# Running the first feed-forward block of the first tile on x·g, with the norm factor applied after the sums, and x and the first weights loaded first

## The chip, the cores and the metric

The kernel runs on all 8 cores of one Trainium2 chip. Each core computes one batch element with its own copy of the program. The time is device time in microseconds of the slowest core. Most executions of one kernel agree closely (the kernel before, seven in one batch: 2812.6 to 2815.0 us), but some fall into a slower state in which the cores of one die (0 to 3, or 4 to 7), sometimes of both, show a lower granted TensorE clock. In one of 3333.07 us, for example, cores 4 to 7 had a mean clock of 0.819 to 0.826, and cores 0 to 3 of 0.992 to 0.994. This text compares undisturbed executions only. Where a trace contains both kinds of core, it uses the undisturbed ones.

## The reference, cut to what matters

```python
D_MODEL, BATCH, SEQ, D_FF = 1024, 8, 4096, 2816

def rmsnorm(x, g):
    y = x * lax.rsqrt(jnp.mean(x * x, axis=-1, keepdims=True) + EPS)
    return y * g

def swiglu(h, w_gate, w_up, w_down):
    return (jax.nn.silu(h @ w_gate) * (h @ w_up)) @ w_down

# x: (8, 4096, 1024) float32
x = x + 0.5 * swiglu(rmsnorm(x, norm_ffn1), ffn1_w_gate, ffn1_w_up, ffn1_w_down)
h = rmsnorm(x, norm_mix)
... # attention branch and spatial-gating ("sgu") branch from h @ w_in, merged by gates
x = x + merged @ w_out
x = x + 0.5 * swiglu(rmsnorm(x, norm_ffn2), ffn2_w_gate, ffn2_w_up, ffn2_w_down)
return rmsnorm(x, norm_final)
```

The norm factor is one number per row of x, so `(x*r*g) @ w` equals `r * ((x*g) @ w)`. That identity is what the change uses.

## The kernel before: the parts that matter

Each core walks over 8 tiles of 512 rows. The weights are float32 in HBM. They arrive through a ring in SBUF, in chunks of up to 1 MB of bf16. A chunk is first loaded with a DMA that casts float32 to bf16, issued by GpSimd. In some tile it is written back to HBM as bf16, and later loads are plain copies issued by SyncE:

```python
def pump():                                     # fills the ring, in the order of use
    ...
    if chunk not in converted:
        u = uses.get(chunk, 0); uses[chunk] = u + 1
        ...
        p.dma("pool", lambda e, ...: e.dma_start(out=dst, in_=src), writes=res, ...)   # casts
        if u >= (first_seen[chunk] * 2) % NREP:                                        # NREP = 3
            converted.add(chunk)
            pending_wb[k] = (chunk, scr, dst, i)     # written back when it is first used
    else:
        p.dma("sp", lambda e, ...: e.dma_start(out=dst, in_=scr), ...)                  # plain
```

For the 19 chunks of the first FFN (11 of gate and up weights, 8 of down weights), this rule writes back 7 chunks in tile 0, 6 in tile 1 and 6 in tile 2.

The norm adds up eight squares and turns the sum into a factor RSTD with one matmul and two ScalarE operations.

```python
def nsq(t, d, eng="pool"):     # square on ScalarE; the running sum ACC on `eng`, GpSimd by default
    ...
    p.add("act", ... AF.Square ...)
    if d < 7:
        p.add(eng, lambda e: e.tensor_tensor(out=ACC[:], in0=ACC[:], in1=buf[:], op=ALU.add), ...)
    else:
        p.add("dve", ... out=ACCR[:] ...)
```

The FFN takes its PSUM banks in pairs, and the pieces of other work ("hooks") run between the groups of matmuls. Four of the eight banks serve all dense products in turn:

```python
def dense_bank():
    b = dn[0] % 4; dn[0] += 1; return b

for f2 in (3, 8, 9, 10, 2, 0, 1, 4, 5, 6, 7):        # 11 weight chunks
    Wc, wres, k = get_slot(("ffs", i, f2))
    for a in range(2):                               # two pairs per chunk
        bg, bu = dense_bank(), dense_bank()
        ...                                          # 8 gate matmuls into bg
        ...                                          # silu: ScalarE (tanh form in the second FFN)
        hook()
        ...                                          # 8 up matmuls into bu
        ...                                          # VectorE: HT = silu(gate) * up
        hook()
...                                                  # then 8 chunks of the down projection

def sgu_mix(t, s):                                   # one of the hooks
    b = dense_bank()                                 # takes the next bank for 8 small matmuls
```

The start of the program, and the hooks of the first FFN of tile 0:

```python
for d in range(8): nsq(0, d, "dve")
nstat()
for d in range(8): napply(0, 0, d)                   # XT = x * g * RSTD
run_all(ffn(0, 0, False, ffn1_hooks(0)))

add_hook(hk, 4, const_loads); add_hook(hk, 8, P(load_x, 1))      # constants, x of tile 1
for i in range(4): add_hook(hk, 20 + 2 * i, P(bias_exp, i))
add_hook(hk, 30, const_ops)                          # 9 us of set-up on VectorE
```

Of the kernel before, what the change touches and what calls it, by code (L numbers as in the profile page):

```python
# [181 lines left out]
def build_nc(n_tiles=NT):  # L182
# [28 lines left out]
    with ExitStack() as st:  # L211
# [5 lines left out]
        def bank(i):  # L217
            return PS[i // 2][:, (i % 2) * 512:(i % 2 + 1) * 512]
# [54 lines left out]
        def run(p, dry):  # L273
# [29 lines left out]
            def pump():  # L303
                while nxt[0] < len(chunk_order) and (general[0] or nxt[0] < fast_len[0]):
                    k = nxt[0]
                    chunk = chunk_order[k]
                    scr, src, ncols = chunk_aps(chunk)
                    ng = -(-ncols // 512)
                    o = cursor[0]
                    if o + ng > NGR:  # L310
                        o = 0
                    if any(a < o + ng and o < b for a, b in live.values()):
                        return
                    nxt[0] += 1
                    cursor[0] = o + ng
                    live[k] = (o, o + ng)
                    res = [("rg", g) for g in range(o, o + ng)]
                    dst = RING[:, o * 512:o * 512 + ncols]
                    W = dst
                    place[k] = (W, res)  # L320
                    if len(scr.shape) == 3:
                        dst = dst.rearrange("p (f c) -> p f c", f=scr.shape[1])
                    i = k % NSEM
                    if chunk not in converted:
                        u = uses.get(chunk, 0)
                        uses[chunk] = u + 1
                        if chunk not in first_seen:
                            first_seen[chunk] = len(first_seen)
                        p.dma("pool", lambda e, dst=dst, src=src: e.dma_start(out=dst, in_=src),
                              writes=res, sem=f"slotq{i}")  # L330
                        if u >= (first_seen[chunk] * 2) % NREP:
                            converted.add(chunk)
                            pending_wb[k] = (chunk, scr, dst, i)
                    else:
                        p.dma("sp", lambda e, dst=dst, scr=scr: e.dma_start(out=dst, in_=scr),
                              reads=[("SCR", chunk)], writes=res, sem=f"slot{i}")
# [28 lines left out]

            dn = [0]

            def dense_bank():
                b = dn[0] % 4
                dn[0] += 1  # L370
                return b

# [89 lines left out]
            def napply(t, which, d):  # L462
# [4 lines left out]
                    out=dst, in0=src, scalar=G4[:, which * 8 + d:which * 8 + d + 1], in1=RSTD[:], op0=ALU.mult, op1=ALU.mult),  # L467
                    reads=[xres, "RSTD", "G4"], writes=[dres])

            def store(t, d):  # L470
                b = t % 3
                p.dma("sp", lambda e: e.dma_start(out=out_d[:, d:d + 2, t * T:(t + 1) * T], in_=X[b][:, d:d + 2, :]),
                      reads=[("X", b, d), ("X", b, d + 1)], writes=[("outd", d)], sem=f"o{d}")

            N_FFN = 2 * NFC + 16

            def ffn(t, i, use_tanh, hooks=None):
                hooks = hooks or {}
                xt, xp, b3 = XT[t % 2], t % 2, t % 3
                piece = 0  # L480

                def hook():
                    nonlocal piece
                    if piece in hooks:
                        hooks[piece]()
                    piece += 1

                for f2 in (3, 8, 9, 10, 2, 0, 1, 4, 5, 6, 7):
                    Wc, wres, k = get_slot(("ffs", i, f2))
                    for a in range(2):  # L490
                        fc = 2 * f2 + a
                        W = Wc[:, a * 2048:(a + 1) * 2048]
                        bg, bu = dense_bank(), dense_bank()
                        for kc in range(8):
                            p.add("pe", lambda e, kc=kc, W=W, bg=bg: e.matmul(  # L495
                                bank(bg), lhsT=W[:, kc * 128:(kc + 1) * 128], rhs=xt[:, kc, :], start=(kc == 0), stop=(kc == 7)),
                                reads=wres + [("XT", xp, kc)], writes=[rb(bg)])
                        buf, bres = tg_buf()
                        if use_tanh:
                            p.add("act", lambda e, buf=buf, bg=bg: e.activation(out=buf[:], in_=bank(bg), func=AF.Tanh, scale=0.5),  # L500
                                  reads=[rb(bg)], writes=[bres])
                            p.add("dve", lambda e, buf=buf, bg=bg: e.scalar_tensor_tensor(  # L502
                                out=buf[:], in0=buf[:], scalar=1.0, in1=bank(bg), op0=ALU.add, op1=ALU.mult),
                                reads=[bres, rb(bg)], writes=[bres])
                        else:
                            p.add("act", lambda e, buf=buf, bg=bg: e.activation(out=buf[:], in_=bank(bg), func=AF.Silu),  # L506
                                  reads=[rb(bg)], writes=[bres])
                        hook()
                        yield
                        for kc in range(8):  # L510
                            p.add("pe", lambda e, kc=kc, W=W, bu=bu: e.matmul(  # L511
                                bank(bu), lhsT=W[:, 1024 + kc * 128:1024 + (kc + 1) * 128], rhs=xt[:, kc, :],
                                start=(kc == 0), stop=(kc == 7)),
                                reads=wres + [("XT", xp, kc)], writes=[rb(bu)])
                        p.add("dve", lambda e, buf=buf, bu=bu, fc=fc: e.tensor_tensor(  # L515
                            out=HT[:, fc, :], in0=bank(bu), in1=buf[:], op=ALU.mult),
                            reads=[rb(bu), bres], writes=[("HT", fc)])
                        if a == 1:
                            free_slot(k)
                        hook()  # L520
                        yield
                fac = 0.25 if use_tanh else 0.5
                for d in range(8):
                    W, wres, k = get_slot(("wds", i, d))
                    by = dense_bank()
                    for part in range(2):
                        for fc in range(part * 11, part * 11 + 11):
                            p.add("pe", lambda e, fc=fc, W=W, by=by: e.matmul(  # L528
                                bank(by), lhsT=W[:, fc * 128:(fc + 1) * 128], rhs=HT[:, fc, :],
                                start=(fc == 0), stop=(fc == NFC - 1)),  # L530
                                reads=wres + [("HT", fc)], writes=[rb(by)])
                        if part == 1:
                            xs = X[b3][:, d, :]
                            p.add("dve", lambda e, by=by, xs=xs: e.scalar_tensor_tensor(  # L534
                                out=xs, in0=bank(by), scalar=fac, in1=xs, op0=ALU.mult, op1=ALU.add),
                                reads=[rb(by), ("X", b3, d)], writes=[("X", b3, d)])
                            free_slot(k)
                        hook()
                        yield
# [347 lines left out]
            def ffn1_hooks(t):  # L887
                hk = {}
                if t == 0:
                    add_hook(hk, 4, const_loads)  # L890
                    add_hook(hk, 30, const_ops)
                    for i in range(4):
                        add_hook(hk, 20 + 2 * i, P(bias_exp, i))
                    add_hook(hk, 8, P(load_x, 1))
                    for d in range(8):
                        add_hook(hk, 16 + 3 * d, P(nsq, 1, d))
                    add_hook(hk, 52, bias_sums)
                    add_hook(hk, 41, nstat)
                    for d in range(8):
                        add_hook(hk, 43 + d, P(napply, 1, 0, d))  # L900
                if t == 1:
                    add_hook(hk, 0, nstat)
                    for d in range(8):
# [32 lines left out]
            def run_all(g):  # L936
                for _ in g:
                    pass

            load_x(0)  # L940
            p.dma("act", lambda e: e.dma_start(out=G4[:], in_=g4_d), writes=["G4"], sem="c0")
            if not dry:
                pump()
            p.add("dve", lambda e: e.memset(ONESR[:].bitcast(F32), 1.0), writes=["ONESR"])
            p.add("dve", lambda e: e.memset(EPSB[:], EPS), writes=["EPSB"])
            p.add("dve", lambda e: e.memset(NHALF[:], -0.5), writes=["NHALF"])
            for d in range(8):
                nsq(0, d, "dve")
            nstat()
            for d in range(8):  # L950
                napply(0, 0, d)
            run_all(ffn(0, 0, False, ffn1_hooks(0)))

            nxt_ffn = ffn(1, 0, True, ffn1_hooks(1))
            for _ in range(4):
# [154 lines left out]
```

## Time and profile before

| | before |
|---|---|
| time, median of the 3 fast runs beside the changed kernel | 2814.84 us |
| TensorE share of the chain that ended last (core 0; 91% on core 5) | 92% |
| first matmul of the first FFN | 24.4 us |
| first FFN of tile 0 done | 163.2 us |
| steady tile (a later tile, measured from a fixed point in it to the same point in the next) | 342.2 us |

The profiled execution of this kernel: cores 0 to 3 had a mean granted clock of 0.93, cores 4 to 7 of 0.994 to 0.995. Cores 4 to 7 took 2802.6 to 2810.0 us here; in seven fast executions of this kernel the same cores took 2800.8 to 2813.5, so they stand for an undisturbed run. All readings below are of core 5. The page (of the slow core 0) says in its part on the chain that ended last (work followed back from the last instruction, so a share of the span and not of busy time):

```profile
PE 92%; DMA 3%; DVE 2%; ACT 1%; issue 1%; POOL 0%; DVEq 0%; ACTq 0%; SPq 0%; POOLq 0%
```

On core 5 the same part gives 91% to TensorE and 4% to DMA. So the program is bound by TensorE. What can be won lies in its gaps. The waits view of TensorE, core 5, names what matmuls waited for (line, releaser: us in total, times, longest):

```profile
PE ps L455 <- DVE ACCR L447: 31.7, 11, 21.1
...
PE ps L495 <- DMA RING<-fsrc: 6.2, 3, 3.8
...
PE ps L511 <- DVE HT L515: 4.7, 2, 2.6
PE ps L495 <- ACT TG L506: 4.3, 2, 3.3
```

The 21.1 us is the start: TensorE has nothing to do until the squares of x are summed. The timeline of TensorE, core 5, shows it (start, duration, line, operation, count; in brackets the idle time before it and what ended that):

```profile
21.14 0.77 PE L455 MATMUL ps<-ACCR,ONESR 128*128 128x512 f32 x1 [21.14 <-DVE ACCR L447]
24.42 5.22 PE L495 MATMUL ps<-XT,RING 128*128 128x512 bf16 x8 [2.52 <-DVE XT L466]
...
35.93 1.89 PE L495 MATMUL ps<-XT,RING 128*128 128x512 bf16 x8
...
107.41 3.45 PE L511 MATMUL ps<-XT,RING 128*128 128x512 bf16 x8 [2.65 <-DVE HT L515]
...
124.75 21.53 PE L528 MATMUL ps<-HT,RING 128*128 128x512 bf16 x99
...
163.19 1.89 PE L495 MATMUL ps<-XT,RING 128*128 128x512 bf16 x8
```

The first chunk runs from 24.4 to 35.9 us, partly at a slow pace. The down projection starts at 124.75 us and the first FFN is done at 163.19 us. A group of eight matmuls takes 1.89 us in most of the trace, but the one at 107.41, after a wait of 2.65 us, takes 3.45: its matmuls start 0.43 us apart instead of 0.216. At the start the spacing of 0.43 us holds from 29.4 to 32.0 us; there the granted clock reads 1.00, so the trace shows the pace but not what sets it. The eight matmuls before that start 0.66 us apart, which is the pace at which VectorE writes XT (eight tiles in 5.39 us), so their spacing is VectorE's and not TensorE's own.

One write-back looks expensive. The chain that ended last, core 5, has this piece (start, duration, what):

```profile
46.21 40.46 DMA ffs<-RING
```

A write-back of 1 MB took 40 us from issue to landing (the median of the 22 such write-backs on this core is 12.5 us), and its ring slot was held for that time.

### The profile page before, as it was taken

To read this page: it belongs to the slowest core of one execution; us is meant where nothing else is said; L and a number is where in the kernel's file an instruction comes from. 1 tells how busy PE (TensorE), PEld (TensorE's weight loads), DVE (VectorE), ACT (ScalarE), POOL (GpSimd) and SP (SyncE) were. 2 spreads that over 40 slices of the span, in tenths; PEclk is the share of its full clock that TensorE was granted. 3 is DMA by queue.
4 is the path that set the end of the run, shared out by engine and by line. 5 is a ranking of instruction groups with operands and counts; after the bars stand their busy time and mean duration, and the time that the engine had idled before them with its cause. 6 is when DMAs were issued, how large, how long until landed. Compare 5 with 4: busy or idle time off the path is not lost.

```text
span 2974.2 us, 38345 instructions; the slowest of 8 cores (2802.6 to 2974.2 us)
## 1 busy us (share of the span) xinstructions
PE 2891.8 (97%) x13034; PEld 1288.2 (43%) x13034; DVE 1248.1 (42%) x1929; ACT 893.9 (30%) x1347; POOL 503.3 (17%) x490
## 2 busy tenths in 40 slices
PE   6899999999999999999999999999999999999997
PEld 2344444444444444444444444444444444444443
DVE  2326343263432644336433464324544255455432
ACT  2323232232322323224232232323323233343221
POOL 0212312112111121111211121111211112102111
PEclk9899889998999999999999999999999999999998
DMA  9988999877777554664344443444334443433352
GB/s 194 189 166 209 176 182 176 176 208 175 176 185 184 169 144 154 176 202 170 133 142 144 161 149 135 149 144 164 139 137 140 144 148 133 141 128 123 128 182 78
DMA packets 112517, 472.41 MB, mean 159 GB/s; under 512 B 9144, under 2 KB 9144, under 8 KB 104128
## 3 DMA queue, kind: packets, MB, share of 16 engines
q1 hardware_dynamic: 90288, 371.71, 36.4%
q0 software_dynamic: 21312, 97.10, 20.6%
q8 instruction: 112, 1.84, 0.2%
q10 hardware_dynamic: 720, 1.07, 0.2%
q14 instruction: 85, 0.70, 0.1%
HBM read 501.92 MB, written 65.01 MB: 191 GB/s over the span
## 4 chain that ended last, share of the span: by engine, by line
PE 92%; DMA 3%; DVE 2%; ACT 1%; issue 1%; POOL 0%; DVEq 0%; ACTq 0%; SPq 0%; POOLq 0%
PE ps L528 22%; PE ps L511 20%; PE ps L495 20%; PE ps L810 8%; PE ps L557 6%; PE ps L820 4%; PE ps L570 3%; PE ps L839 3%; PE ps L701 2%; PE ps L687 2%; DMA ffs<-RING 1%; DMA RING<-fsrc 1%; DMA wos<-RING 0%; PE ps L644 0%; PE ps L455 0%
## 5 line engine op out<-in xcount | busy, mean ns | idle before, releaser
L495 PE MATMUL ps<-XT,RING 128*128 128x512 bf16 x2816 | 706.7, 396 | 6.8 <-DVE XT L466 2.5
L511 PE MATMUL ps<-XT,RING 128*128 128x512 bf16 x2816 | 706.8, 397 | 6.3 <-DVE HT L515 6.3
L528 PE MATMUL ps<-HT,RING 128*128 128x512 bf16 x2816 | 660.7, 399 | 0.0
L528 PEld LDWEIGHTS ps<-HT,RING 128*128 128x128 bf16 x2816 | 285.2, 102 | 362.7 <-issue 145.2
L515 DVE TENSOR_TENSOR HT<-ps,TG 128x512 bf16<-128x512 f32 x352 | 241.1, 685 | 466.8 <-PE ps L511 419.0
L511 PEld LDWEIGHTS ps<-XT,RING 128*128 128x128 bf16 x2816 | 281.4, 101 | 351.3 <-issue 121.2
L495 PEld LDWEIGHTS ps<-XT,RING 128*128 128x128 bf16 x2816 | 281.8, 101 | 350.5 <-issue 119.6
L444 POOL TENSOR_TENSOR ACC<-ACC,TG 128x512 f32<-128x512 f32 x186 | 239.8, 1289 | 1075.4 <-ACT TG L441 1074.3
L441 ACT ACTIVATE TG<-X 128x512 f32<-128x512 f32 x224 | 140.2, 627 | 547.5 <-DVE X L534 453.4
L534 DVE SCALAR_TENSOR_TENSOR X<-ps,X 128x512 f32<-128x512 f32 x128 | 88.4, 692 | 424.7 <-PE ps L528 420.8
L810 PE MATMUL ps<-XT,RING 128*128 128x512 bf16 x1024 | 261.1, 401 | 0.0
L506 ACT ACTIVATE TG<-ps 128x512 f32<-128x512 f32 x176 | 105.0, 597 | 449.0 <-PE ps L495 435.4
L691 ACT ACTIVATE E<-ps 128x1024 bf16<-128x1024 f32 (+1 forms) x240 | 168.4, 702 | 197.3 <-PE ps L687 174.3
L732 POOL TENSOR_SCALAR TG<-TG 128x512 bf16<-128x512 f32 x64 | 98.8, 1543 | 587.3 <-DVE TG L721 577.6
L502 DVE SCALAR_TENSOR_TENSOR TG<-TG,ps 128x512 f32<-128x512 f32 x176 | 119.7, 680 | 168.5 <-ACT TG L500 145.3
L500 ACT ACTIVATE TG<-ps 128x512 f32<-128x512 f32 x176 | 105.1, 597 | 266.6 <-PE ps L495 236.1
L557 PE MATMUL ps<-XT,RING 128*128 128x512 bf16 x768 | 178.2, 395 | 0.0
L694 DVE TENSOR_TENSOR E<-E,EB 128x1024 bf16<-128x1024 bf16 (+1 forms) x240 | 127.5, 531 | 94.9 <-ACT E L691 93.9
L824 DVE SCALAR_TENSOR_TENSOR TG<-TG,ps 128x512 f32<-128x512 f32 x128 | 87.8, 687 | 182.1 <-PE ps L820 155.3
L810 PEld LDWEIGHTS ps<-XT,RING 128*128 128x128 bf16 x1024 | 103.8, 102 | 135.1 <-issue 60.2
L815 ACT ACTIVATE TG<-ps,BG 128x512 f32<-128x512 f32 x128 | 87.5, 687 | 241.1 <-PE ps L810 241.0
L466 DVE SCALAR_TENSOR_TENSOR XT<-X,G,RSTD 128x512 bf16<-128x512 f32 x192 | 135.6, 746 | 30.9 <-ACT RSTD L459 30.9
(91 smaller groups left out, 1937.5 us busy)
## 6 DMA issues: line engine op xcount, KB each, us to landing
RING<-ffs SPq DMA_DIRECT2D x131, 1024.0 KB, 5.0
RING<-wds SPq DMA_DIRECT2D x97, 704.0 KB, 4.4
RING<-fsrc POOLq DMA_DIRECT2D x45, 1024.0 KB, 13.4
RING<-mgs SPq DMA_DIRECT2D x48, 768.0 KB, 4.3
RING<-wis SPq DMA_DIRECT2D x29, 1024.0 KB, 4.8
ffs<-RING SPq DMA_DIRECT2D x22, 1024.0 KB, 12.2
RING<-wd POOLq DMA_DIRECT2D x31, 704.0 KB, 11.2
out<-X SPq DMA_DIRECT2D x32, 512.0 KB, 4.1
```

Of the source, the lines that this page charges most:

```text
L441: p.add("act", lambda e: e.activation(out=buf[:], in_=src, func=AF.Square, scale=1.0 / 32.0), reads=[xres], writes=[bres])
L444: p.add(eng, lambda e: e.tensor_tensor(out=ACC[:], in0=ACC[:], in1=buf[:], op=ALU.add), reads=["ACC", bres], writes=["ACC"])
L466: p.add("dve", lambda e: e.scalar_tensor_tensor(out=dst, in0=src, scalar=G4[:, which * 8 + d:which * 8 + d + 1], in1=RSTD[:], op0=ALU.mult ...
L495: p.add("pe", lambda e, kc=kc, W=W, bg=bg: e.matmul(bank(bg), lhsT=W[:, kc * 128:(kc + 1) * 128], rhs=xt[:, kc, :], start=(kc == 0), stop= ...
L502: p.add("dve", lambda e, buf=buf, bg=bg: e.scalar_tensor_tensor(out=buf[:], in0=buf[:], scalar=1.0, in1=bank(bg), op0=ALU.add, op1=ALU.mul ...
L511: p.add("pe", lambda e, kc=kc, W=W, bu=bu: e.matmul(bank(bu), lhsT=W[:, 1024 + kc * 128:1024 + (kc + 1) * 128], rhs=xt[:, kc, :], start=(k ...
L515: p.add("dve", lambda e, buf=buf, bu=bu, fc=fc: e.tensor_tensor(out=HT[:, fc, :], in0=bank(bu), in1=buf[:], op=ALU.mult), reads=[rb(bu), b ...
L528: p.add("pe", lambda e, fc=fc, W=W, by=by: e.matmul(bank(by), lhsT=W[:, fc * 128:(fc + 1) * 128], rhs=HT[:, fc, :], start=(fc == 0), stop= ...
L557: p.add("pe", lambda e, kc=kc, W=W, b=b, cc=cc: e.matmul(bank(b), lhsT=W[:, kc * 512 + cc * 128:kc * 512 + (cc + 1) * 128], rhs=XT[t % 2][ ...
L691: p.add("act", lambda e: e.activation(out=ee, in_=PS[2][:].rearrange("p (h c) -> p h c", h=2)[:, :, 0:n], func=AF.Exp), reads=[rb(4), rb(5 ...
L694: p.add("dve", lambda e: e.tensor_tensor(out=ee, in0=ee, in1=EB[:, 2 * hp:2 * hp + 2, u0:u0 + n], op=ALU.mult), reads=[("E", i % 2), ("EB" ...
L810: p.add("pe", lambda e, kc=kc, W=W, bgt=bgt, j=j: e.matmul(bank(bgt), lhsT=W[:, j * 1024 + kc * 128:j * 1024 + (kc + 1) * 128], rhs=XT[t % ...
```

## The change

Intent: chunk 0 of tile 0's first FFN runs k by k on x·g as x lands, with no norm before it. The norm factor scales the sums as they leave PSUM: VectorE multiplies the gate sums by RSTD, ScalarE applies silu, VectorE multiplies by RSTD again, and the product with the up sums follows. x and the first weight chunk are loaded first, the latter in four quarters. No chunk is written back in tile 0. Set-up work moves later, and so do the squares, the norm factor and x·g of tile 1 (not shown below). The raw FFN turns over six PSUM banks instead of four.

```diff
+                        if k == 0:                       # first chunk in four quarters
+                            for j in range(4): ...
+                        else:
+                            p.dma("pool", ...,
+                                  reads=[("X", 0, 7)] if k == 1 else (), writes=res, ...)   # waits for x
-                        if u >= (first_seen[chunk] * 2) % NREP:
+                        if u >= (first_seen[chunk] % 2 + 1 if first_seen[chunk] < 19 else (first_seen[chunk] * 2) % NREP):
...
+            def nraw(t, which, d): ...                   # XT = x * g
...
+                    elif raw:
+                        p.add("dve", ... out=buf[:], in0=bank(bg), in1=RSTD[:], op=ALU.mult ...)
+                        p.add("act", ... out=buf[:], in_=buf[:], func=AF.Silu ...)
+                        p.add("dve", ... out=buf[:], in0=buf[:], in1=RSTD[:], op=ALU.mult ...)
...
+                n_dense[0] = 6 if raw else 4
                 for f2 in (3, 8, 9, 10, 2, 0, 1, 4, 5, 6, 7):
+                    by_k = raw and f2 == 3
+                    banks = [dense_bank() for _ in range(4)]
+                    if by_k:
+                        for kc in range(8):
+                            nraw(t, 0, kc)
+                            for j in range(4): mm(banks[j], Wc, wres, j, kc)
+                            ...
                     for a in range(2):
-                        bg, bu = dense_bank(), dense_bank()
+                        bg, bu = banks[2 * a], banks[2 * a + 1]
...
-                    add_hook(hk, 4, const_loads)
+                    add_hook(hk, 20, const_loads)
-                        add_hook(hk, 20 + 2 * i, P(bias_exp, i))
+                        add_hook(hk, 36 + 2 * i, P(bias_exp, i))
-                    add_hook(hk, 8, P(load_x, 1))
+                    add_hook(hk, 14, P(load_x, 1))
...
-            for d in range(8):
-                nsq(0, d, "dve")
-            nstat()
-            for d in range(8):
-                napply(0, 0, d)
-            run_all(ffn(0, 0, False, ffn1_hooks(0)))
+            run_all(ffn(0, 0, False, ffn1_hooks(0), raw=True))
```

Note the line `banks = [...]`: it is needed for the k-by-k chunk, but it stands in the code of every FFN of every tile.

## The prediction

> All readings are of core 5 (clock 0.995; die 0 was slow in the profiled run).
>
> **What bounds the kernel.** TensorE. In the waits view its matmuls wait about 39 us in the first tile's first FFN (0 to 163 us) and almost nothing from 180 to 530 us. Those 39 us: 21.1 us before the first matmul (the norm's sums; x lands over 18.7 us because five weight casts share the DMA), 2.5 us for the norm factor, 6.2 us for weights, 4.3 and 4.7 us for evictions held up by setup work. The first matmuls go at 0.66, then 0.43 us each instead of 0.216 us[...]. DMA share is mostly 0.9 to 1.04 over the first 200 us. From queue bytes over queue share, a casting weight chunk (1 MB) costs about 6.5 us, a plain megabyte 2.7 us; TensorE uses a chunk in 6.9 us.
>
> **What the change does.**
> 1. No norm wait: chunk 0 runs by k as x lands. I expect the first matmul at 11-15 us, chunk 0 done at 20-23 us (before: 36). Gain there about 15 us.
> 2. No write-backs in tile 0. Before, one took 40 us (46 to 86 us, chain of waits) and held a ring slot. This goes.
> 3. Against it: later chunks start only when x has landed, and the second x tile and bias table (3.9 MB with the constants), no longer behind a write-back, compete with chunks 1 to 3. I expect waits there, chunk 3 at about 46 us.
> 4. Every gate costs VectorE three 0.69 us operations around one 0.60 us ScalarE one, in order: about 3.2 us per pair, against 3.46 us of matmuls. No slack remains for setup. The constant setup (9.6 us of VectorE, 97 to 106.6 us before) waits for the small spatial-gating weights, now queued behind chunk 9 (estimate: landing at 84-90 us). After it four bias exponentials, each with two 1.28 us table loads, stretch four pairs to about 5.3 us. From the setup's end the chain needs 0.7 + 6.4 + 21.2 us, then 35 us of down projection: first FFN done at 157-165 us, against 163-166 before. Most of the early gain is given back.
> 5. Tile 1: seven chunks that came back as bf16 are casts again, with four more write-backs: about 31 us more DMA work. Before, I count 141 us of DMA work from 163 to 330 us; after, about 172. The ring's five chunks should hide this; up to 5 us of weight waits possible. Tile 2 gets about 16 us more, into idle DMA.
>
> **On the critical path:** the first 163 us; nothing later unless the DMA falls behind.
>
> **Prediction:** 2809 us, range 2796 to 2819 (before: 2814.84). Faster by over 2% 0.01, within 2% 0.97, slower by over 2% 0.02. Even removing all 39 us would be 1.4%.
>
> **What would show each step.** Timeline: first matmul near 11-15 us; chunk 0's end. Waits: matmuls on weights for chunks 1 to 3. Groups: two new norm-factor multiplications, 22 each, near 0.69 us. Timeline: constant setup starting at 80-90 us, TensorE then waiting on VectorE; the down projection's first bank waiting for the last hidden rows. Windows: DMA share near 1 from 165 to 330 us.
>
> **What would make it wrong.** If the small weights land early, or table loads overlap better, the first FFN ends near 150 us and the gain is 10 to 18 us. If the extra casts in tile 1 make TensorE wait, the result is 10 us or more slower; write-backs could also hold ring slots there as in tile 0.

## More of the kernel before

A ruler for the rest: the first matmul of the gates' merge (line 810) occurs once per tile. Its start on core 5 in tiles 0 and 2:

```profile
330.97 1.89 PE L810 MATMUL ps<-XT,RING 128*128 128x512 bf16 x8
...
1015.42 1.89 PE L810 MATMUL ps<-XT,RING 128*128 128x512 bf16 x8
```

Below, **T0** is the start of the first merge, **D1** and **D2** the next two distances from merge to merge (here 342.3 and 342.2), and a **steady tile** one of the later ones (342.2). Tile 0's first FFN lies in T0, and most of the repeated weight casts in T0, D1 and D2.

## The result, and the profile after

The changed kernel took 2842.66 us (median of 4 runs, 2841.12 to 2845.6, all undisturbed) against 2814.84 us (median of the 3 fast runs of before). The ratio is 1.0099, with a 95% interval of 1.0079 to 1.0119: some 28 us slower, outside the predicted range and with the wrong sign. The result was correct. All ratios here are the mean time of one kernel's fast runs over that of the other's of the same rounds, so not quite the ratio of the medians quoted.

The same view of the chain that ended last, on the slowest core (2):

```profile
PE 84%; DMA 9%; DVE 2%; ACT 2%; issue 2%; POOL 0%; SPq 0%; ACTq 0%; DVEq 0%; POOLq 0%
```

DMA rose from 3% (4% on core 5) to 9% of the chain. The waits view of TensorE, core 2:

```profile
PE ps L504 <- DMA RING<-fsrc: 29.3, 6, 13.9
PE ps L464 <- DVE ACCR L456: 21.6, 10, 9.8
PE ps L571 <- DVE TG L517: 11.3, 1, 11.3
...
PE ps L504 <- DVE HT L527: 6.0, 1, 6.0
PE ps L687 <- ACT TG L523: 5.7, 6, 0.9
...
PE ps L687 <- DVE TG L513: 3.6, 2, 1.8
```

The wait for the sum of squares at the start is gone. In its place are 29.3 us of waits for weights, 13.86 of them before the first matmul, and two waits of 6 and 11 us behind VectorE. A norm wait of 9.8 us belongs to a later tile. The two L687 rows (the small matmuls of sgu_mix) are new: their 9.3 us have no counterpart in before. (Line numbers differ between the two kernels.) The timeline of TensorE, core 2:

```profile
13.86 0.59 PE L504 MATMUL ps<-XT,RING 128*128 128x512 bf16 x1 [13.86 <-DMA RING<-fsrc]
...
23.25 8.64 PE L504 MATMUL ps<-XT,RING 128*128 128x512 bf16 x29 [3.71 <-DMA RING<-fsrc]
...
37.17 22.97 PE L504 MATMUL ps<-XT,RING 128*128 128x512 bf16 x94 [5.05 <-DMA RING<-fsrc]
62.88 36.42 PE L504 MATMUL ps<-XT,RING 128*128 128x512 bf16 x165 [2.74 <-DMA RING<-fsrc]
105.32 1.01 PE L504 MATMUL ps<-XT,RING 128*128 128x512 bf16 x2 [6.03 <-DVE HT L527]
...
130.98 7.87 PE L571 MATMUL ps<-HT,RING 128*128 128x512 bf16 x22 [11.27 <-DVE TG L517]
...
172.62 1.89 PE L504 MATMUL ps<-XT,RING 128*128 128x512 bf16 x8
```

The first matmul came 10.6 us earlier (13.86 against 24.42). But chunk 1 could start only at 37.17, against 35.93 before (on core 5 of the changed kernel: first matmul 11.52, chunk 1 at 39.20). The whole head start was gone after one chunk. Then VectorE stopped TensorE twice, and the first FFN ended at 172.6 us (169.9 to 172.7 over the eight cores) against 163.2.

The first merges of tiles 0 and 2, core 5, to compare with the same core before:

```profile
338.81 1.89 PE L853 MATMUL ps<-XT,RING 128*128 128x512 bf16 x8
...
1040.26 1.89 PE L853 MATMUL ps<-XT,RING 128*128 128x512 bf16 x8
```

On core 5 the changed kernel is 7.8 us late at the first of these (338.81 against 330.97), and 24.8 us late at the second (1040.26 against 1015.42). In medians over the undisturbed cores (4 of before, 8 of after):

| us | T0 | D1 | D2 | steady tile | last of the distances | third to eighth merge |
|---|---|---|---|---|---|---|
| before | 333.0 | 342.6 | 342.8 | 342.2 | 218.1 | 1586.8 |
| after | 340.5 | 345.6 | 353.1 | 343.2 | 220.0 | 1592.8 |
| difference | +7.5 | +3.0 | +10.3 | +1.0 | +1.9 | +6.0 |

(The last distance is shorter because no next tile runs beside it.) The differences T0, D1, D2 and the last column add up to 26.8 us. That is nearly all of the loss. Only 7.5 us of it lies where the change was meant to work, so the later columns needed experiments. They differ in kind. Between the first and the second merge the waits view of core 2 has one new wait of some size, 3.4 us for weights (`RING<-wisrc`). Between the second and the third it has no wait for weights at all, but 13.6 us behind the norm's sum.

### Why D2 grew: a queue on GpSimd

The timeline of GpSimd, VectorE and TensorE around 705 us, core 2:

```profile
702.25 0.57 POOL L336 DMA_DIRECT2D RING<-mgsrc  x1 [8.72 <-DMA wds<-RING]
702.83 1.27 POOL L453 TENSOR_TENSOR ACC<-ACC,TG 128x512 f32<-128x512 f32 x1
...
704.28 0.69 DVE L456 TENSOR_TENSOR ACCR<-ACC,TG 128x512 fp32r<-128x512 f32 x1 [13.23 <-POOL ACC L453]
...
705.22 0.77 PE L464 MATMUL ps<-ACCR,ONESR 128*128 128x512 f32 x1 [9.79 <-DVE ACCR L456]
```

GpSimd issues the casting loads and also adds the squares, in one order. Here its next load wanted a ring slot whose data was still being written back (`wds<-RING`). GpSimd stood for 8.72 us, the addition behind it came late, VectorE waited for the addition, and TensorE waited 9.79 us for the norm. Those late write-backs and casts are the change's: it moved them out of tile 0 into tiles 1 and 2.

### Why T0 grew: VectorE

The timeline of VectorE, core 2, first in a quiet stretch, then through the set-up:

```profile
37.92 0.68 DVE L517 TENSOR_TENSOR TG<-ps,RSTD 128x512 f32<-128x512 f32 x1
39.43 0.69 DVE L520 TENSOR_TENSOR TG<-TG,RSTD 128x512 f32<-128x512 f32 x1 [0.83 <-ACT TG L519]
...
40.85 0.69 DVE L517 TENSOR_TENSOR TG<-ps,RSTD 128x512 f32<-128x512 f32 x1
...
87.90 0.69 DVE L527 TENSOR_TENSOR HT<-ps,TG 128x512 bf16<-128x512 f32 x1
...
95.30 0.48 DVE L400 MEMSET WST<- 64x512 bf16 x1 [4.05 <-DMA WST<-wst]
...
104.50 0.67 DVE L527 TENSOR_TENSOR HT<-ps,TG 128x512 bf16<-128x512 f32 x1
```

A pair costs VectorE 2.93 us from one L517 to the next (37.92 to 40.85), in strict order, against 3.46 us of matmuls. The set-up began at 95.30, after 4.05 us of waiting for the small gating weights, and the next hidden rows were written at 104.50, 16.6 us after those at 87.90. Only 0.5 us of slack per pair was there to catch up with (3.46 minus 2.93), and soon the bias exponentials took that too.

The small weights were issued by GpSimd at 71.18 us, directly behind a 1 MB cast (chunk load at 70.50), and used at 95.30:

```profile
71.18 0.58 POOL L396 DMA_DIRECT2D WST<-wst  x1
```

In the DMA view of core 2 the loads of this queue landed in the order of their issue: the cast issued at 60.68 took 26.8 us to landing (87.5), the cast at 70.50 took 22.9 (93.4), these small weights, issued at 71.18, took 23.9 (95.1), and the cast at 77.41 took 25.2 (102.6). The 24 us for this small load agree with a load that stands behind big ones in its own queue. Sharing the engines with another queue is not the cause: in the DMA view of core 2 from 71.2 to 83 us GpSimd's queue alone kept the engines busy (packets, MB, share of the 16 engines), while the queue of the plain loads moved no packet, and from 83 to 95.3 us it took 1.7%:

```profile
q0 software_dynamic: 519, 2.01, 103.0%
```

### The profile page after: what moved, and what is told of

It is laid out like the page before. It is cut to its first block, busy times and chain, and to the rows that moved or that the text cites. A ratio compares the mean times of both kernels' runs of the same rounds, so it can differ in the third digit from the quotient of the medians.

```text
span 2844.0 us, 38131 instructions; the slowest of 8 cores (2821.9 to 2844.0 us)
## 1 busy us (share of the span) xinstructions
PE 2710.8 (95%) x12775; PEld 1248.6 (44%) x13034; DVE 1262.3 (44%) x1973; ACT 891.7 (31%) x1345; POOL 511.3 (18%) x503
## 3 DMA queue, kind: packets, MB, share of 16 engines
q1 hardware_dynamic: 88208, 362.86, 37.3%
q0 software_dynamic: 23696, 105.95, 22.7%
HBM read 510.77 MB, written 65.01 MB: 202 GB/s over the span
## 4 chain that ended last, share of the span: by engine, by line
PE 84%; DMA 9%; DVE 2%; ACT 2%; issue 2%; POOL 0%; SPq 0%; ACTq 0%; DVEq 0%; POOLq 0%
PE ps L504 36%; PE ps L571 20%; PE ps L853 7%; PE ps L600 6%; PE ps L863 4%; PE ps L613 4%; DMA ffs<-RING 3%; PE ps L882 3%; PE ps L744 2%; PE ps L730 2%; DMA RING<-fsrc 1%; DMA wds<-RING 1%; DMA RING<-wisrc 1%; DMA WST<-wst 1%; DMA X<-xT 1%
## 5 line engine op out<-in xcount | busy, mean ns | idle before, releaser
L504 PE MATMUL ps<-XT,RING 128*128 128x512 bf16 x5507 | 1259.4, 381 | 42.6 <-DMA RING<-fsrc 29.3
L504 PEld LDWEIGHTS ps<-XT,RING 128*128 128x128 bf16 x5632 | 547.1, 98 | 669.9 <-issue 48.7
L571 PE MATMUL ps<-HT,RING 128*128 128x512 bf16 x2759 | 614.8, 380 | 14.2 <-DVE TG L517 11.3
L571 PEld LDWEIGHTS ps<-HT,RING 128*128 128x128 bf16 x2816 | 275.2, 98 | 342.0 <-issue 16.0
L853 PE MATMUL ps<-XT,RING 128*128 128x512 bf16 x1006 | 242.1, 381 | 1.1
L523 ACT ACTIVATE TG<-ps 128x512 f32<-128x512 f32 x154 | 91.9, 597 | 379.4 <-PE ps L504 357.8
L511 ACT ACTIVATE TG<-ps 128x512 f32<-128x512 f32 x176 | 105.1, 597 | 240.8 <-PE ps L504 210.4
L600 PE MATMUL ps<-XT,RING 128*128 128x512 bf16 x755 | 167.7, 379 | 0.7
L853 PEld LDWEIGHTS ps<-XT,RING 128*128 128x128 bf16 x1024 | 100.0, 98 | 122.2 <-issue 4.9
L613 PE MATMUL ps<-RING,XT 128*128 128x512 bf16 x501 | 121.5, 396 | 6.8 <-DMA RING<-wisrc 3.4
L600 PEld LDWEIGHTS ps<-XT,RING 128*128 128x128 bf16 x768 | 75.2, 98 | 90.6
```

The costliest lines, as they stand in the source:

```text
L504: p.add("pe", lambda e: e.matmul(bank(b), lhsT=W[:, j * 1024 + kc * 128:j * 1024 + (kc + 1) * 128], rhs=xt[:, kc, :], start=(kc == 0), sto ...
L571: p.add("pe", lambda e, fc=fc, W=W, by=by: e.matmul(bank(by), lhsT=W[:, fc * 128:(fc + 1) * 128], rhs=HT[:, fc, :], start=(fc == 0), stop= ...
L600: p.add("pe", lambda e, kc=kc, W=W, b=b, cc=cc: e.matmul(bank(b), lhsT=W[:, kc * 512 + cc * 128:kc * 512 + (cc + 1) * 128], rhs=XT[t % 2][ ...
L613: p.add("pe", lambda e, kc=kc, W=W, b=b, s=s: e.matmul(bank(b), lhsT=XT[t % 2][:, kc, s * 128:(s + 1) * 128], rhs=W[:, kc * 512:(kc + 1) * ...
L853: p.add("pe", lambda e, kc=kc, W=W, bgt=bgt, j=j: e.matmul(bank(bgt), lhsT=W[:, j * 1024 + kc * 128:j * 1024 + (kc + 1) * 128], rhs=XT[t % ...
```

## The experiments

T0, D1, D2 below are medians over the cores of the one profiled execution of each kernel with a mean granted clock of at least 0.9865. They proved more useful than whole-run times: in some executions two cores of a die had a mean clock of 0.98 instead of 0.99, and the run took some 20 us longer (experiment 2: 2846.15 us with cores 6 and 7 at 0.980, against 2823.31 and 2821.66). The windows view shows where this mean comes from. In experiment 1 core 0 (mean 0.982) had a clock of 0.82 from 40 to 80 us, 0.81 from 80 to 120 and from 140 to 208, and 1.00 from 208 to 340; core 2 of the same die (mean 0.992) had 1.00 from 40 to 80. So this core lost its time in the first tile, that is in T0; cores with such a mean are left out. A median hides one thing: the time of a run is that of its slowest core, and D1 and D2 scatter over the cores. The experiments ran on three chips, each batch beside the kernel before on the same chip; ratios are taken within a batch.

### Theories

- Bank order: the extra 1.0 us per steady tile comes from taking four banks at the start of a chunk. The rival: it comes from the changed DMA traffic.
- Set-up: the loss at T0 comes from the set-up in the middle of a VectorE-bound stretch. The rival: from the raw start itself, or from the new write-back rule.
- Write-backs: the loss in D1 and D2 comes from the new write-back rule. Within it: through the GpSimd queue, or through plain lack of DMA time.

### 1 and 2. Bank order, undone and done alone

```diff
 # e1: changed kernel, only the k-by-k chunk takes four banks
-                    banks = [dense_bank() for _ in range(4)]
+                    banks = [dense_bank() for _ in range(4)] if by_k else None
-                        bg, bu = banks[2 * a], banks[2 * a + 1]
+                        bg, bu = (banks[2 * a], banks[2 * a + 1]) if by_k else (dense_bank(), dense_bank())
```

> The changed kernel, but each chunk's PSUM banks are taken two at a time again (as before the change) in every FFN except for the first chunk of the raw one. Theory: the changed kernel takes all four banks of a chunk at its start, so that the spatial-gating product, which takes its bank in the middle of a chunk, gets a bank whose gate is not yet read, and TensorE waits 0.9 to 1.8 us in each tile; this costs 1.0 us in each steady tile (343.2 instead of 342.2 us from merge to merge) and about 8 us in all. It expects 2834 us (8 us below the changed kernel), 342.2 us per steady tile, and no wait of the spatial-gating matmuls on the gate's evictions. Rival: the extra microsecond per tile is an effect of the shifted loads; then 2842 us and 343.2 us per tile stay.

```diff
 # e2: kernel before, with four banks at the start of each chunk
+                    banks = [dense_bank() for _ in range(4)]
-                        bg, bu = dense_bank(), dense_bank()
+                        bg, bu = banks[2 * a], banks[2 * a + 1]
```

> The kernel before, with only one thing of the change: all four banks of a chunk are taken at its start. Theory (bank order): about 8 us slower than before, 2823 us, with 343.2 us per steady tile and waits of 0.9 and 1.8 us before the spatial-gating matmuls. Rival (loads): no difference, 2815 us.

Measured: e1 has steady tiles of 342.2 us and a last distance of 218.1, as before; e2 has 343.2 and 220.0, as after. The rest is 1586.9 us in e1 and 1592.8 in e2. In e2 the waits view of TensorE, core 5, has the new rows (L645 is sgu_mix there), and e1 has none like them:

```profile
PE ps L645 <- ACT TG L507: 5.7, 6, 0.9
...
PE ps L645 <- DVE TG L503: 3.6, 2, 1.8
```

The totals, 5.7 and 3.6 us, are those of after to the digit. The bank-order theory holds, both ways, for the steady tiles. (In tiles 0 to 2, which other things disturb, e1 has T0 337.0, D1 347.4 and D2 348.6.) When sgu_mix runs between two groups of a chunk, `dense_bank()` gives it the next bank in turn. With pairs, that is one whose data left long ago. With four taken at the chunk's start, it is one of the current chunk's own, whose gate sums ScalarE is just reading.

The whole-run times tell this less well. e1's fast runs were 2845.74, 2852.49, 2847.62 and 2837.04 us, ratio 1.0113 (1.0088 to 1.0138) to before, no better than the changed kernel: cores at the clock of 0.98 set the time (in the profiled execution core 0 at 0.982 was the slowest, with 2844.1 us). e2's were 2823.31, 2821.66 and 2846.15, ratio 1.0071 (1.0021 to 1.0122). So the whole-run time of e1 is a miss.

### 3 and 4. The write-back rule, undone and done alone

```diff
 # e3: changed kernel with the old rule
-if u >= (first_seen[chunk] % 2 + 1 if first_seen[chunk] < 19 else (first_seen[chunk] * 2) % NREP):
+if u >= (first_seen[chunk] * 2) % NREP:
 # e4: kernel before with the new rule
-if u >= (first_seen[chunk] * 2) % NREP:
+if u >= (first_seen[chunk] % 2 + 1 if first_seen[chunk] < 19 else (first_seen[chunk] * 2) % NREP):
```

> The changed kernel with the old rule for write-backs (a third of the chunks at the first use, so seven in the first tile; fewer casts later). Theory: the new rule puts more casts and write-backs into tiles 1 and 2, so that DMA issues on GpSimd wait for ring slots and hold up the norm sums queued behind them on the same engine (the 4 to 10 us wait at 690 us); the first tile is held by the chain of VectorE and ScalarE, so write-backs there cost little. It expects 2828 us (8 to 20 us below the changed kernel), merges 344 us apart at the second and third, and the first merge within 4 us of the changed kernel's 340 us. Rival: write-backs in the first tile are what stalled the kernel before, and bringing them back delays the first merge by 8 us or more, giving 2840 us or above.

> The kernel before with only the new rule for write-backs. Theory: the first tile gains 5 to 10 us (no ring slot held by a write-back: the weight waits at 64 to 100 us go), and the second and third merge are 5 to 18 us late; together 2815 to 2828 us. Rival (the rule is a gain by itself, and the loss in tiles 1 and 2 comes from the other parts of the change): 2805 to 2810 us, merges 342 us apart throughout.

| us | T0 | D1 | D2 | sum | ratio to before (95%) |
|---|---|---|---|---|---|
| before | 333.0 | 342.6 | 342.8 | 1018.4 | 1 |
| e4: before, new rule | 323.6 | 347.9 | 348.0 | 1019.5 | 1.0040 (1.0023 to 1.0057) |
| after | 340.5 | 345.6 | 353.1 | 1039.2 | 1.0099 (1.0079 to 1.0119) |
| e3: after, old rule | 349.9 | 343.3 | 343.6 | 1036.8 | 1.0085 (1.0069 to 1.0102) |

(Here and below the sum is that of the three medians, not a median of sums.) The rule moves the same thing in both kernels: without write-backs T0 is 9.4 us shorter, and D1 and D2 together are 10.5 (e4) and 11.8 us (after against e3) longer. By itself it gives back all it gains, and on the slowest core more: e4's runs are 11 us slower than before, and D2 lies between 342.2 and 357.4 us over its cores. In e3 the expectation that I favoured missed at T0, which got 9.4 us worse under the old rule; the rival was right. Its total, 2837 us, missed the expected 2828 for that reason; D1 and D2 came out at 343 to 344 as expected. The write-back theory holds in its first half: the rule causes the loss in D1 and D2.

### 5 and 6. The set-up moved, and the raw start undone

```diff
 # e5: set-up into the down projection, when the hidden rows are done
-                    add_hook(hk, 30, const_ops)
+                    add_hook(hk, D1 + 3, const_ops)
-                        add_hook(hk, 36 + 2 * i, P(bias_exp, i))
+                        add_hook(hk, D1 + 6 + 2 * i, P(bias_exp, i))
-                    add_hook(hk, D1 + 11, bias_sums)
+                    add_hook(hk, D1 + 13, bias_sums)
 # e6: changed kernel, but with the norm first
-            run_all(ffn(0, 0, False, ffn1_hooks(0), raw=True))
+            for d in range(8): nsq(0, d, "dve")
+            nstat()
+            for d in range(8): napply(0, 0, d)
+            run_all(ffn(0, 0, False, ffn1_hooks(0)))
```

(`D1` in this code is the number of the hook at which the down projection starts.)

> The changed kernel with the constant setup and the four bias exponentials moved from the middle of the first FFN's gate and up products into its down projection (bias sums two pieces later). Theory: the waits of 4 to 6 us near 103 us and of 11 us near 129 us are the setup work inserted into a VectorE-ScalarE chain that the raw evictions have filled; both go, the first merge comes 12 to 17 us earlier (about 325 us instead of 340), and the rest stays: 2826 to 2832 us. Rival: the first tile is bound by the DMA of its weights, and the waits only turn into waits for weights; then the first merge stays above 335 us.

> The changed kernel with only its first idea undone: the first FFN again waits for the norm and runs on x times g times the norm factor, with plain evictions on four banks; new write-back rule, order of first loads, hooks and banks stay. Theory: since chunk 1 lands only at 37 to 39 us, the early start buys nothing, and without the raw evictions the chain has slack again: first merge 325 to 332 us (8 to 15 us earlier than the changed kernel), 2830 us. Rival: the raw start is a real gain of about 10 us that other parts of the change hide; then the first merge is at 345 us or later.

| us | T0 | D1 | D2 | ratio to before (95%) |
|---|---|---|---|---|
| after | 340.5 | 345.6 | 353.1 | 1.0099 (1.0079 to 1.0119) |
| e5: set-up late | 319.8 | 349.6 | 351.9 | 1.0066 (1.0022 to 1.0111) |
| e6: norm first | 331.6 | 350.0 | 352.0 | 1.0134 (1.0103 to 1.0165) |

Moving the set-up gives 20.7 us at T0 (12 to 17 were expected), the largest effect of any single edit to the changed kernel: on core 5 the down projection starts at 109.5 us (before 124.75; 130.98 on core 2 of the changed kernel), and the first FFN ends at 148.2 us. The set-up theory holds. Undoing the raw start (and with it the raw evictions and the six banks) at the changed kernel's set-up place also gains, 8.9 us: with the set-up there, the raw start is worse than none. The whole-run ratio of e6 is not comparable: in all its fast runs cores 2 and 3 had a clock of 0.982 to 0.985. In both, part of the earlier T0 is lost again in D1 (+4 us).

### 7. The norm's additions off GpSimd

```diff
 # e7: changed kernel, squares of tiles 1 and later added on VectorE in the down projection
-                    add_hook(hk, D1 + 2 * d + 1, P(nsq, t, d))
+                    add_hook(hk, D1 + 2 * d + 1, P(nsq, t, d, "dve" if t else "pool"))
```

> The changed kernel with the norm's partial sums of the first FFN of tiles 1 and later added on VectorE instead of GpSimd. Theory: the 3 to 10 us wait of the norm matmul near 695 us comes from these additions queueing on GpSimd behind weight loads that wait for ring slots; it goes, and the third merge follows the second by 344 to 348 us instead of 348 to 360: 2832 us. Rival: the additions are late because x itself or ScalarE's squares are late; then the wait stays within 2 us of what it was.

Measured on 4 undisturbed cores: D2 345.0 us (343.2 to 346.9) instead of 353.1; T0 340.4 and D1 347.6, not better. The ratio was 1.0073 (1.0049 to 1.0097). So 8 of the 10 us of D2 came through the GpSimd queue, not through a lack of DMA time. The waits of TensorE behind the norm's sum between the second and the third merge, core 2, changed kernel first, then e7, fell with it:

```profile
PE ps L464 <- DVE ACCR L456: 13.6, 2, 9.8
```

```profile
PE ps L464 <- DVE ACCR L456: 2.9, 1, 2.9
```

An addition costs 1.27 us on GpSimd and 0.69 on VectorE here. But the speed was not the point (0.6 us per addition); the order in the queue was, with its stall of 8.72 us.

### 8. All three repairs together

e8 is e1, e5 and e7 in one kernel.

> The changed kernel with three repairs: banks in pairs, setup in the down projection, norm sums of later tiles on VectorE. If the three causes are separate their gains add: 8 + 14 + 6 us, first merge 324 us, 342.2 us per steady tile, 2812 to 2818 us, about as fast as the kernel before. If the loads of tiles 1 and 2 are the true limit, the earlier first merge is lost again by the third one, and it stays at 2825 us or more.

Measured: T0 322.1, D1 353.4 (349.2 to 360.4), D2 345.8, steady tiles 342.2. Fast runs: 2827.39 and 2820.28 us. Against e5, T0 is kept, the bank loss and most of the D2 loss are gone, but D1 rose to 353. The gains do not simply add: TensorE now arrives earlier at tile 1's weights, and waits there for them. The waits view of core 2 shows it: between its first and second merge (322.3 and 682.7 us) TensorE waited 14.0 us for weights of five kinds; core 5 of the kernel before had no such wait from 320 to 690. The DMA share alone would not tell: it is 1.01 to 1.03 in every 40 us from 320 to 520 on both cores.

### 9 to 12. Variants of the repaired kernel

Each is e8 with one edit.

```diff
 # e9: the old rule
+if u >= (first_seen[chunk] * 2) % NREP:
 # e10: write-backs spread over tiles 1, 2 and 3
+if u >= (first_seen[chunk] % 3 + 1 if first_seen[chunk] < 19 else (first_seen[chunk] * 2) % NREP):
 # e11: that for the 11 gate and up chunks; the old rule for the down chunks
+if u >= (first_seen[chunk] % 3 + 1 if first_seen[chunk] < 11 else (first_seen[chunk] * 2) % NREP):
 # e12: chunk 1 no longer waits for x
-                                  reads=[("X", 0, 7)] if k == 1 else (), writes=res, ...)
+                                  writes=res, ...)
```

> The kernel with three repairs (banks in pairs, late setup, norm sums of later tiles on VectorE) and the old write-back rule. It separates the raw start from the write-back rule. Theory: with the setup out of the way seven write-backs in the first tile cost 6 to 10 us there (first merge 328 to 334 us), and the second and third merge follow at 342 to 344 us as in the kernel before; 2808 to 2816 us. Rival: the raw start needs the rule; write-backs hold ring slots as before and the first merge is at 338 us or later, 2820 us.

> The three repairs, and the first FFN's chunks written back at their second, third or fourth use in turn (none at the first): six to seven write-backs in each of tiles 1 to 3. Theory: from 160 to 530 us the DMA is the limit (TensorE waits for weights there in the repaired kernel), and ten write-backs in tile 1 are four too many; with six the second merge follows the first by 346 to 350 us instead of 353, the third by at most 346: 2806 to 2814 us. Rival: it is the nineteen casts, not the write-backs, and nothing changes in tile 1, while tile 2 gets worse: 2815 to 2825 us.

> The three repairs, with the spread rule for the eleven gate and up chunks alone and the old rule for the eight down chunks (three of them written back in the first tile). Theory: three plain reloads in tile 1 save about 7 us of DMA there for 6 us in the first tile, so the first merge is 2 to 5 us later than with the spread rule and the second interval 5 us shorter: 2804 to 2812 us. Rival: as the spread rule or slower.

> The three repairs, without the order x before chunk 1: chunks 1 to 4 are issued at once, as before the change. Theory: the bytes are the same, so holding chunk 1 back until x has landed buys nothing: chunk 0 may start up to 4 us later, chunk 1 comes up to 8 us earlier, and the first merge moves by at most 3 us either way (322 us). Rival (x first is what makes the early start): first merge 5 us or more later.

| us | casts, write-backs in tile 1 (first FFN) | T0 | D1 | D2 | sum | fast runs |
|---|---|---|---|---|---|---|
| e8 | 19, 10 | 322.1 | 353.4 | 345.8 | 1021.3 | 2827.39, 2820.28 |
| e9 | 12, 6 | 351.4 | 344.0 | 342.9 | 1038.3 | 2840.51, 2831.85, 2836.58, 2836.07 |
| e10 | 19, 7 | 317.0 | 355.4 | 342.9 | 1015.3 | 2818.91, 2815.93 |
| e11 | 16, 7 | 321.5 | 347.2 | 342.7 | 1011.4 | 2814.61, 2804.92, 2806.86 |
| e12 | 19, 10 | 318.9 | 359.9 | 344.9 | 1023.7 | 2819.8, 2815.88, 2817.94, 2818.02 |

**e9**: my favoured expectation missed again. Even with the set-up out of the way, T0 is 351.4 us with the old rule. The timeline of core 0 around 117 us shows a path:

```profile
116.81 0.57 POOL L336 DMA_DIRECT2D RING<-wd  x1 [32.49 <-DMA ffs<-RING]
...
118.77 0.63 ACT L450 ACTIVATE TG<-X 128x512 f32<-128x512 f32 x1 [19.71 <-POOL ACC L453]
...
120.02 0.69 DVE L520 TENSOR_TENSOR TG<-TG,RSTD 128x512 f32<-128x512 f32 x1 [16.85 <-ACT TG L519]
```

A write-back held a ring slot. GpSimd stood 32.49 us before the load that needed the slot. The additions of tile 1's squares stood behind it, so ScalarE, which needs their buffers, stopped for 19.71 us in front of the next square, the silu behind that square came late, and VectorE waited 16.85 us for it. In the raw form every pair goes VectorE, ScalarE, VectorE, so this reached TensorE, which then waited 7.70 us before its down projection:

```profile
131.24 6.90 PE L571 MATMUL ps<-HT,RING 128*128 128x512 bf16 x22 [7.70 <-DVE TG L517]
```

The old rule costs 29.3 us at T0 here (against e8), the largest effect of all runs. That the raw form makes it so dear is argued from this path; the old rule with the norm first was not run in the repaired kernel.

**e10** has three write-backs fewer in tile 1 than e8 and the same casts. D1 did not fall (355.4; its cores lie between 344.9 and 366.4). D2 did (342.9). This points to the rival: in D1 it is the casts, not the write-backs. (Its second half, a worse tile 2, did not come.) **e11** has three casts fewer in tile 1, and keeps three write-backs of down chunks in tile 0. D1 fell to 347.2 and T0 stayed. **e12** lets chunk 1 come earlier. T0 gained 3 us, about what its theory allowed, and D1 lost 6.5, which its expectation did not have. Ratios to before: e9 1.0048 (1.0024 to 1.0072), e11 0.9945 (0.9916 to 0.9974), e12 0.9986 (0.9963 to 1.0008). e11 is faster than both kernels: by about 15 us against before by its ratio, or 12 by the means of the fast runs of that batch.

### 13. Is the raw start worth anything in the repaired kernel?

e13 is e11 with the edit of e6: the norm comes first (and the raw evictions and the six banks go with the raw start), and everything else of e11 stays.

> The fastest repaired kernel (banks in pairs, late setup, norm sums on VectorE, mixed write-back rule) with the raw start undone: the first FFN waits for the norm. It measures what the raw start itself is worth once nothing stands in its way. Theory: the DMA brings chunk 1 at 38 us in either case, so the raw start is worth at most 3 us: first merge 317 to 325 us, 2803 to 2810 us. Rival: it is worth the 8 us or more by which its first matmuls come earlier: first merge at 328 us or later, 2814 us.

Measured: T0 320.5 (318.0 to 323.6; 321.5 in e11), D1 about 350, D2 343.4, fast runs 2812.74, 2804.74 and 2804.44 us, ratio 0.9941 (0.9917 to 0.9965). It is as fast as e11 without the change's main idea. The timelines of TensorE on core 0 say why. In e11:

```profile
38.99 15.73 PE L504 MATMUL ps<-XT,RING 128*128 128x512 bf16 x64 [6.46 <-DMA RING<-fsrc]
...
112.25 4.91 PE L571 MATMUL ps<-HT,RING 128*128 128x512 bf16 x22
```

In e13:

```profile
27.25 11.61 PE L504 MATMUL ps<-XT,RING 128*128 128x512 bf16 x32 [2.52 <-DVE XT L475]
42.71 72.04 PE L504 MATMUL ps<-XT,RING 128*128 128x512 bf16 x313 [3.85 <-DMA RING<-fsrc]
114.58 4.91 PE L571 MATMUL ps<-HT,RING 128*128 128x512 bf16 x22
```

With the norm first, TensorE starts 15 us later than e11's 12 us, but then waits less for weights. The down projections start at 112.25 and 114.58 us on this core, and at 112.57 and 112.64 on core 5. The start is set by when the weights of chunk 1 and after land, and starting the first chunk sooner is worth 0.1 to 2.3 us of it.

## Why the prediction was wrong, point by point

1. **"First matmul at 11-15 us" held; "chunk 0 done at 20-23 us" and "Gain there about 15 us" failed.** The first matmul came at 13.86 us on core 2. Chunk 0 was done at 31.5 us, because its four quarters landed one after another until 23 us and the 29 matmuls that were left ran slowly (8.64 us). Then TensorE waited 5.05 us for chunk 1, which started at 37.17 us; before, at 35.93. The gain at chunk 1 was about nothing. Experiment 13 shows that in the repaired kernel the norm wait could be put back for free. I had taken the wait for the norm as lost time, although weights were being loaded under it (of the 16 DMA engines' time from 0 to 21.1 us, their queue took 50.5% in the kernel before, core 5).
2. **"No write-backs in tile 0 ... This goes" held.** It is worth 9.4 us at T0 (experiments 3 and 4).
3. **Waits on chunks 1 to 3 were expected; on core 2 only the one on chunk 1 came, and one on chunk 4.** Chunk 1 waited 5.05 us and chunk 4 2.74 us; chunks 2 and 3 ran through (94 recorded matmuls in one stretch from 37.17). "Chunk 3 at about 46 us" was too early: two chunks of 6.9 us after 37.17, it is about 51.
4. **The VectorE mechanism was right, its size was off.** The pair cost 2.93 us (predicted 3.2), the set-up began at 95.30 instead of 84-90 us, and the waits were 6.03 and 11.27 us. The first FFN ended at 169.9 to 172.7 us, not 157-165. Put the prediction's own sum beside core 2. The set-up began 5 to 11 us late. From its end at about 104.5 us to the down projection at 130.98 took 26.5 us (predicted 0.7 + 6.4 + 21.2, so 28.3). The down projection took 41.6 us (172.62 minus 130.98), not 35; it took 38.4 in the kernel before, and here its first 22 matmuls took 7.87 us instead of 4.91 (experiment 5), at half the granted clock after the wait (0.50 from 130.98 to 137 us). So two terms were mis-sized, the start of the set-up and the down projection. Experiment 5 puts the whole cost of this placing at 20.7 us of T0. That is against the same kernel with the set-up late; in the kernel before, too, evictions held up by set-up cost TensorE 4.3 and 4.7 us.
5. **"Tile 2 gets about 16 us more, into idle DMA" failed.** The loss in D2 was the largest, 10.3 us. The reasoning counted DMA time only. The extra loads also went into GpSimd's queue, in front of the norm's additions (experiment 7: 8 of the 10 us). For tile 1 I allowed "up to 5 us of weight waits"; D1 grew by 3.0 us, 1 of which is bank order. (The plain rate of the prediction, 2.7 us per MB, is also low: queue share over queue bytes gives 2.9 on core 5 of before.) The windows view shows the DMA side as predicted, near 1 in tile 1. Its last two columns are DMA share and GB/s; first before, core 5, from 240 to 320 us, then after, core 2:

```profile
240.00:280.00 40.00, 39.89 (x199) 18.91 (x198) 28.85 (x42) 14.23 (x24) 11.87 (x10) 1.00 0.80 186
280.00:320.00 40.00, 40.00 (x193) 18.46 (x192) 20.86 (x28) 8.59 (x15) 17.39 (x18) 1.00 0.97 198
```

```profile
240.00:280.00 40.00, 37.89 (x197) 18.06 (x200) 28.75 (x46) 13.80 (x22) 8.56 (x9) 1.00 0.99 192
280.00:320.00 40.00, 39.79 (x194) 18.82 (x196) 24.48 (x32) 10.81 (x18) 16.49 (x18) 1.00 1.03 219
```

6. **"Nothing later unless the DMA falls behind" failed.** After the first merge the kernel lost 3.0 + 10.3 + 6.0 = 19.3 of the 26.8 us. The bank order is a change in every FFN of every tile, and costs 1.0 us per steady tile, 6.0 us from the third merge on (experiments 1 and 2). It stood in the diff, and I did not ask who else calls `dense_bank()`.

So two steps failed. The gain of step 1 did not come, and the path "the first 163 us; nothing later" was too short: 19.3 us of the loss lie after it. Without the gain the rest of the sum had only costs: set-up 20.7 us in T0 against 9.4 won by the write-backs, GpSimd's queue 8 us, bank order 6 us and a little in T0 to D2. These terms were measured in different kernels and do not add exactly (experiment 8). What stays open is how D1 splits between casts and write-backs. That TensorE waits there for weights is read from the traces; that it is the casts rests on e10 and e11 with cores that spread by more than 10 us. I had named the risk ("the result is 10 us or more slower" if tile 1's casts or write-backs bite) but given it too little weight.

## What to carry to other kernels

Before removing a wait at the start, ask what else becomes ready during it: if the data for the next step lands no earlier, the wait only moves (here the first matmul came 10.6 us earlier, and the second chunk 1.2 us later). When a change allocates from a shared rotation (banks, buffers, queue places), look at everyone else who draws from that rotation, in all stages, since a microsecond per tile in a place that the change did not mean to touch outlives its gain (here 6.0 us from the third merge on). And an engine that both issues transfers and computes passes the wait before an issue on to its computations (GpSimd here: 8.72 us, and 32.49 us in experiment 9); count places in its queue, not only bytes.

## Costs that these runs show

- A cast during DMA. In the changed kernel (core 2) the casting queue took 22.7% of 2844.0 us for 105.95 MB landed, that is 6.1 us per MB; the plain queue took 37.3% for 362.86 MB, 2.9 us per MB. Counted by the float32 bytes read, twice those landed, the two rates are nearly the same (328 and 342 GB/s). So, as an estimate from these two rates, a cast from float32 to bf16 costs what its source bytes cost. (That the queue's figure counts landed bytes fits the page's total: 362.86 - 65.01 written + 2 x 105.95 is 509.75 MB, and 510.77 MB were read from HBM.)
- A load issued by an engine that also computes. The two issues quoted above took GpSimd 0.57 us each, but it stood for 8.72 us before the one, and for 32.49 us before the other (experiment 9), with additions of 1.27 us behind it.
- A clock that differs within a die. In the profiled run of experiment 1 cores 0 and 1 had mean clocks of 0.982 and 0.984, and cores 2 and 3 of the same die 0.992 and 0.989. In that of the changed kernel all eight cores had 0.987 to 0.991.
- A third user of a rotation of PSUM banks that is handed a bank whose sums are still being read: 1.0 us per steady tile in experiments 1 and 2 (343.2 against 342.2).
